# Shifting the weight tiles of a layer's first half by 384 bytes in SBUF

## The chip, the cores and the metric

The kernel runs on one NeuronCore of a Trainium2 chip. The metric is the device time of one execution in microseconds (us); three executions before the change took 1393.44 to 1394.48 us, with a median of 1394.12 us.

## What is computed

One layer of a trunk, `x + W_out [ya, yb, yc]`, with 256 tokens and 4096 channels in float32. The three branches read the same normalised input through one combined input projection, and a final RMSNorm follows.

```python
h = _rmsnorm(x, norm_g[l])
proj = h @ w_in[l]                       # 256 x 4096 by 4096 x 11008
a_val, a_glu, a_gate, b_u, b_v, b_gate, c_in, c_gate = jnp.split(proj, SPLITS, axis=-1)
ya = _conformer_conv_branch(...) * jax.nn.silu(a_gate)   # 31 taps, LayerNorm, 1536 x 1536
yb = _gmlp_chunk_branch(...) * jax.nn.silu(b_gate)       # position mixing per head
yc = _pool_branch(...) * jax.nn.silu(c_gate)             # trailing means, 320 x 320 per group
y = jnp.concatenate([ya, yb, yc], axis=-1) @ w_out[l]    # 256 x 4096 by 4096 x 4096
x = x + y
return _rmsnorm(x, final_g)
```

## The kernel before

Each operand of a large product is split into two parts, `hi` (rounded to the type that TensorE multiplies, `F32R`) and `lo` (the rest), and a product is the sum of three matmuls, `act_hi x w_hi`, `act_hi x w_lo` and `act_lo x w_hi`. In `rows_product` these are lines 338, 339 and 340. The activations are the stationary operand: tiles `act` of 2048 bytes in each partition, in which hi and lo of the two halves of the tokens lie 512 bytes apart. The weights are the moving operand, 512 columns at a time in most places.

`stream` (called from `project_rows`) reads weights in blocks of 1 MB into `w_raw` tiles on the SP queue (L205), and `split` makes of every 1024 columns the `w_hi` part (ScalarE, L218) and the `w_lo` part (VectorE, L219). `feed` keeps two split pairs ahead of the pair that TensorE multiplies; one pair serves twelve matmuls of 512 columns. Beside each split, `run_beside` records some of the elementwise work of the branches (convolution L525, gates, norms), so the order on each engine is fixed when the program is built.

The program has two halves, by where the weights lie in SBUF:

- **First half**: `first_group`, the other column groups of the input projection, the C branch's small products (`use_c`, 320 columns wide) and the A branch's pointwise projection. Its weight tiles come from the pool `wpool` at the right end of SBUF: four `w_raw` of 8192 bytes, three `w_hi` and three `w_lo` of 4096 bytes. The branch tiles `h_a` and `a_gate` lie in the pool `gate`, to the left of it.
- **Second half**: `first_columns` (the first 512 columns of the output projection, by the same `stream` and the same lines 338 to 340, into the same PSUM pool `ps_acc`), then three times `paired_columns` (products L875 to L877 into the banks `q`), then the last 512 columns (`use_last`, again L338 to L340, in the order 512, 256, 256 columns at first). Its weight tiles come from the pool `wpool2` on the left, right behind the activations, with three `w_raw` and five `w_hi` and `w_lo` each.

The activations lie in the same 32 places in both halves. Byte addresses in a partition, as the built program has them:

| tiles | address | modulo 512 | modulo 2048 |
|---|---|---|---|
| `act` (32 tiles, step 2048; four parts of 512 bytes each) | 19552 to 83040 | 96 | 1120 |
| `w_hi`, `w_lo` of the first half, before | 204768 to 225248, step 4096 | 480 | 2016 |
| `w_hi`, `w_lo` of the first half, after | 204384 to 224864, step 4096 | 96 | 1632 |
| `w_hi`, `w_lo` of the second half, before and after | 109664 to 146528, step 4096 | 96 | 1120 |
| `w_raw` of the first half, before and after | 172000 to 196576; 171616 to 196192 | 480; 96 | 2016; 1632 |
| `h_a`, `a_gate`, before and after | 158272; 157888 | 64; 192 | 576; 192 |

So a weight part of the first half lies 384 bytes past a multiple of 512 from every activation part before the change; one of the second half lies at a multiple of 512 from them, and since the four parts of an `act` tile are 512 bytes apart, all four distances modulo 2048 (0, 512, 1024, 1536) occur there.

Of the 512-column products, the first half holds 1416 at each of the lines 338, 339 and 340 (4248 matmuls); 64 at each of these lines belong to `first_columns` and 32 to the last columns. The matmuls of 256 columns are 64 at each line in the first half (the last chunk of `b_v`) and 64 in the last columns.

Of the kernel before, what the change touches and what calls it, by code (L numbers as in the profile page):

```python
# [22 lines left out]
F32 = mybir.dt.float32  # L23
# [5 lines left out]
P = 128  # L29
# [65 lines left out]
def trunk(ctx: ExitStack, tc: tile.TileContext, x, xt, params, w1, wv, w2, w_pw, w_c, w_o, wst, bbias, blg, blb, fg, out):  # L95
# [3 lines left out]
    acts = ctx.enter_context(tc.tile_pool(name="acts", bufs=1))  # L99

    front_ctx, ps_ctx = ExitStack(), ExitStack()
    weights = {"pool": front_ctx.enter_context(tc.tile_pool(name="wpool", bufs=1, side="right")), "raw": 4, "parts": 3}
    gate = front_ctx.enter_context(tc.tile_pool(name="gate", bufs=1, side="right"))
    ps_acc = ps_ctx.enter_context(tc.tile_pool(name="ps_acc", bufs=6, space=PSUM))
# [1023 lines left out]
```

## Time and profile before

| what | value |
|---|---|
| median of three executions | 1394.12 us |
| the profiled execution | 1392.27 us, span 1390.5 us |
| TensorE busy | 99% of the span, 6224 records |
| VectorE busy | 75% |
| ScalarE busy | 49% |
| granted TensorE clock | 1.00 of full speed, 0.88 in the last of 40 slices |
| moved by DMA | 281 MB, 202 GB/s in the mean |

PE is TensorE, PEld its loads of the stationary operand, DVE VectorE, ACT ScalarE, POOL GpSimd, SP the queue that issues most DMAs. L339 is line 339 of the kernel. The matmuls are pipelined: the duration of a record is longer than the step from one start to the next, and steps are what the time is made of.

### The profile page before, as it was taken

How to read it: one execution, taken by the hardware profiler on the slowest of the kernel's cores; microseconds unless marked ns; L12 is line 12 of the kernel's file. 1: busy time of each engine (PE TensorE's matmuls, PEld its weight loads, DVE VectorE, ACT ScalarE, POOL GpSimd, SP SyncE). 2: the span in 40 equal slices, each digit the busy share in tenths (PEclk: the TensorE clock that was granted, in tenths of full speed). 3: DMA queues.
4: the chain of work that ended last, by engine and by line, in shares of the span. 5: the costliest groups of instructions: out<-in, count | busy, mean ns of one | idle time of the engine just before them, and what ended most of it. 6: DMA issues, size and time to landing. Idle time of an engine off the chain costs nothing.

```text
span 1390.5 us, 16340 instructions
## 1 busy us (share of the span) xinstructions
PE 1378.2 (99%) x6224; PEld 1133.2 (81%) x6224; DVE 1036.0 (75%) x1468; ACT 675.7 (49%) x806; POOL 5.7 (0%) x52
## 2 busy tenths in 40 slices
PE   9999999999999999999999999999999999999996
PEld 7888888888888888888888888888888888888886
DVE  7458888888888888776445844456668999999974
ACT  7653444434445434554344334445554565655651
POOL 0000000000000000000000000000000000000000
PEclk9999999999999999999999999999999999999998
DMA  9965555555556555555555555554656666666663
GB/s 341 335 255 186 195 182 182 185 185 199 187 195 195 190 198 183 182 182 185 176 183 182 184 190 197 187 181 135 225 212 219 232 214 218 215 212 210 225 224 121
DMA packets 56591, 281.01 MB, mean 202 GB/s; under 512 B 8640, under 2 KB 12096, under 8 KB 31168
## 3 DMA queue, kind: packets, MB, share of 16 engines
q1 hardware_dynamic: 56368, 279.95, 57.5%
q8 instruction: 48, 0.79, 0.2%
q14 instruction: 31, 0.25, 0.0%
q10 hardware_dynamic: 144, 0.02, 0.0%
HBM read 275.75 MB, written 4.19 MB: 201 GB/s over the span
## 4 chain that ended last, share of the span: by engine, by line
PE 99%; DVE 1%; ACT 0%; issue 0%; POOL 0%; ACTq 0%; POOLq 0%
PE ps_acc L338 25%; PE ps_acc L339 25%; PE ps_acc L340 25%; PE q L875 6%; PE q L876 6%; PE q L877 6%; PE q L339 1%; PE q L338 1%; PE q L340 1%; PE ps_aux L315 1%; PE ps_aux L391 0%; PE ps_aux L613 0%; PE ps_aux L276 0%; DVE xn L999 0%; ACT ps_acc L841 0%; DVE w_lo L219 0%
## 5 line engine op out<-in xcount | busy, mean ns | idle before, releaser
L219 DVE TENSOR_TENSOR w_lo<-w_raw,w_hi 128x1024 fp32r<-128x1024 f32 (+1 forms) x495 | 589.0, 1195 | 307.5 <-ACT w_hi L218 305.9
L218 ACT CAST w_hi<-w_raw 128x1024 fp32r<-128x1024 f32 (+1 forms) x495 | 505.0, 1027 | 581.9 <-PE ps_acc L340 506.5
L338 PE MATMUL ps_acc<-w_hi,act 128*128 128x512 f32 (+2 forms) x1568 | 611.9, 391 | 0.0
L339 PE MATMUL ps_acc<-w_lo,act 128*128 128x512 f32 (+2 forms) x1568 | 610.6, 389 | 0.0
L340 PE MATMUL ps_acc<-w_hi,act 128*128 128x512 f32 (+2 forms) x1568 | 610.4, 389 | 0.0
L339 PEld LDWEIGHTS ps_acc<-w_lo,act 128*128 128x128 f32 x1568 | 295.7, 189 | 64.5 <-DVE w_lo L219 0.8
L340 PEld LDWEIGHTS ps_acc<-w_hi,act 128*128 128x128 f32 x1568 | 295.6, 189 | 64.4
L338 PEld LDWEIGHTS ps_acc<-w_hi,act 128*128 128x128 f32 x1568 | 295.6, 189 | 64.2 <-ACT act L295 0.4
L525 DVE SCALAR_TENSOR_TENSOR c_a<-h_a,par,c_a 128x256 f32<-128x256 f32 x360 | 153.5, 477 | 0.0
L875 PE MATMUL q<-w_hi,act 128*128 128x512 f32 x264 | 102.9, 390 | 0.7 <-ACT ps_acc L841 0.7
L876 PE MATMUL q<-w_lo,act 128*128 128x512 f32 x264 | 102.8, 389 | 0.0
L877 PE MATMUL q<-w_hi,act 128*128 128x512 f32 x264 | 102.8, 389 | 0.0
L218 ACT CAST w_hi<-w_sums 128x1024 fp32r<-128x1024 f32 x48 | 50.6, 1054 | 56.3 <-DVE w_sums L950 28.5
L219 DVE TENSOR_TENSOR w_lo<-w_sums,w_hi 128x1024 fp32r<-128x1024 f32 x48 | 58.1, 1220 | 2.6 <-ACT w_hi L218 1.7
L875 PEld LDWEIGHTS q<-w_hi,act 128*128 128x128 f32 x264 | 49.6, 188 | 11.5 <-ACT ps_acc L841 1.2
L877 PEld LDWEIGHTS q<-w_hi,act 128*128 128x128 f32 x264 | 49.6, 188 | 10.3
L876 PEld LDWEIGHTS q<-w_lo,act 128*128 128x128 f32 x264 | 49.6, 188 | 10.2
L877 PE MATMUL q<-w_hi,combo 128*128 128x512 f32 x96 | 37.4, 389 | 0.0
L876 PE MATMUL q<-w_lo,combo 128*128 128x512 f32 x96 | 37.4, 389 | 0.0
L875 PE MATMUL q<-w_hi,combo 128*128 128x512 f32 x96 | 37.0, 389 | 0.0
L339 PE MATMUL q<-w_lo,act 128*128 128x256 f32 (+1 forms) x96 | 30.7, 320 | 0.0
L338 PE MATMUL q<-w_hi,act 128*128 128x256 f32 (+1 forms) x96 | 30.7, 319 | 0.0
(147 smaller groups left out, 614.8 us busy)
## 6 DMA issues: line engine op xcount, KB each, us to landing
w_raw<-in_w_dram SPq DMA_DIRECT2D x149, 1024.0 KB, 4.8
w_raw<-in_w_o_dram SPq DMA_DIRECT2D x96, 512.0 KB, 4.8
w_raw<-in_wv_dram SPq DMA_DIRECT2D x20, 1024.0 KB, 4.8
w_raw<-in_w_o_dram SPq DMA_DIRECT2D x16, 1024.0 KB, 5.1
w_raw<-in_w_pw_dram SPq DMA_DIRECT2D x9, 1024.0 KB, 4.8
x_rows<-in_x_dram SPq DMA_DIRECT2D x4, 1024.0 KB, 6.7
xn<-in_x_dram SPq DMA_DIRECT2D x8, 512.0 KB, 8.1
out_dram<-xn SPq DMA_DIRECT2D x6, 512.0 KB, 3.3
```

The costliest lines, as they stand in the source:

```text
L218: nc.scalar.copy(out=hi[:, w], in_=raw[:, w])
L219: nc.vector.tensor_tensor(out=lo[:, w], in0=raw[:, w], in1=f32(hi[:, w]), op=ALU.subtract)
L315: nc.tensor.transpose(ps[:, c * P : (c + 1) * P], rows[:, c, m * P : (m + 1) * P], ident)
L338: nc.tensor.matmul(ps[:, :w], lhsT=act[:, c, 0], rhs=hi, start=f, stop=False)
L339: nc.tensor.matmul(ps[:, :w], lhsT=act[:, c, 0], rhs=lo, start=False, stop=False)
L340: nc.tensor.matmul(ps[:, :w], lhsT=act[:, c, 1], rhs=hi, start=False, stop=l)
L525: nc.vector.scalar_tensor_tensor(out=c_a[:, m], in0=src, scalar=w, in1=c_a[:, m], op0=ALU.mult, op1=ALU.add)
L875: nc.tensor.matmul(ps, lhsT=ahi, rhs=hi, start=f, stop=False)
L876: nc.tensor.matmul(ps, lhsT=ahi, rhs=lo, start=False, stop=False)
L877: nc.tensor.matmul(ps, lhsT=alo, rhs=hi, start=False, stop=l)
```

## The change

One tile of 96 float32 (384 bytes in each partition) is taken at the right end of SBUF before the weight pool. Nothing reads or writes it.

```diff
     front_ctx, ps_ctx = ExitStack(), ExitStack()
+    ctx.enter_context(tc.tile_pool(name="edge", bufs=1, side="right")).tile([P, 96], F32, name="edge")
     weights = {"pool": front_ctx.enter_context(tc.tile_pool(name="wpool", bufs=1, side="right")), "raw": 4, "parts": 3}
     gate = front_ctx.enter_context(tc.tile_pool(name="gate", bufs=1, side="right"))
```

What stands at the right end, `wpool` and `gate`, moves down by 384 bytes; nothing else moves. The two built programs have the same 10083 instructions in the same order with the same waits; the addresses alone differ.

## Rows read from the trace of the kernel before

**Rows 1.** The page: engines' busy time, and the chain that ended last by engine.
```profile
PE 1378.2 (99%) x6224; PEld 1133.2 (81%) x6224; DVE 1036.0 (75%) x1468; ACT 675.7 (49%) x806; POOL 5.7 (0%) x52
...
PE 99%; DVE 1%; ACT 0%; issue 0%; POOL 0%; ACTq 0%; POOLq 0%
```

**Rows 2.** Stretches: us, busy time and records of each engine, clock, DMA share, GB/s.
```profile
core 0: us, PE busy (x) PEld busy (x) DVE busy (x) ACT busy (x) POOL busy (x), PEclk, DMA share, GB/s
105.00:345.00 240.00, 240.00 (x1043) 194.94 (x1042) 198.98 (x322) 100.30 (x104) 0.00 (x0) 1.00 0.53 186
800.00:940.00 140.00, 140.00 (x604) 113.61 (x603) 67.67 (x62) 58.35 (x61) 0.00 (x0) 1.00 0.53 188
1050.00:1088.00 38.00, 38.00 (x169) 31.51 (x168) 32.28 (x65) 17.95 (x21) 0.00 (x0) 1.00 0.81 279
1110.00:1250.00 140.00, 140.00 (x619) 116.00 (x618) 135.41 (x150) 83.40 (x93) 0.00 (x0) 1.00 0.63 214
```

**Rows 3.** Line 339 from 800 to 940 us: ns min/median/max.
```profile
L339 PE MATMUL ps_acc<-w_lo,act x202: 390/393/405, 799.7 to 939.9; 128*128 128x512 f32 x101
```

**Rows 4.** Line 339 from 1050 to 1088 us, in `first_columns`: ns min/median/max.
```profile
L339 PE MATMUL ps_acc<-w_lo,act x57: 388/389/390, 1049.7 to 1087.8; 128*128 128x512 f32 x57
```

**Rows 5.** Groups of TensorE, whole span, shapes apart: xcount | busy us, mean ns.
```profile
L338 PE MATMUL ps_acc<-w_hi,act 128*128 128x512 f32 x1480 | 586.0, 397 | 0.0
...
L338 PE MATMUL q<-w_hi,act 128*128 128x256 f32 x64 | 18.1, 282 | 0.0
L338 PE MATMUL ps_acc<-w_hi,act 128*128 128x256 f32 x64 | 18.0, 282 | 0.0
...
L391 PE MATMUL ps_aux<-ident,hv 128*128 128x128 f32 x44 | 5.8, 272 | 0.0
L613 PE MATMUL ps_aux<-v,ws_sb 128*128 128x256 f32 x20 | 5.7, 389 | 0.0
...
L315 PE MATMUL ps_aux<-ident,a_gate 128*128 128x128 f32 x24 | 4.6, 274 | 0.0
L315 PE MATMUL ps_aux<-ident,c_gate 128*128 128x128 f32 x20 | 4.1, 278 | 0.0
L315 PE MATMUL ps_aux<-ident,u_b 128*128 128x128 f32 x20 | 3.0, 272 | 0.0
```

**Rows 6.** Timeline of TensorE behind a stall in `paired_columns`: start us, us, instruction.
```profile
1091.20 0.51 PE L875 MATMUL q<-w_hi,act 128*128 128x512 f32 x1 [0.74 <-ACT ps_acc L841]
1091.55 0.40 PE L876 MATMUL q<-w_lo,act 128*128 128x512 f32 x1
...
1094.33 0.39 PE L876 MATMUL q<-w_lo,act 128*128 128x512 f32 x1
...
1095.91 0.39 PE L877 MATMUL q<-w_hi,act 128*128 128x512 f32 x1
```

**Rows 7.** Groups of TensorE from 1340 to 1362 us, shapes apart.
```profile
L338 PE MATMUL q<-w_hi,act 128*128 128x512 f32 x16 | 6.3, 396 | 0.0
```

**Rows 8.** Timeline of TensorE in the first half, from 826 us.
```profile
826.00 0.40 PE L338 MATMUL ps_acc<-w_hi,act 128*128 128x512 f32 x1
826.24 0.41 PE L339 MATMUL ps_acc<-w_lo,act 128*128 128x512 f32 x1
826.48 0.40 PE L340 MATMUL ps_acc<-w_hi,act 128*128 128x512 f32 x1
```

**Rows 9.** Waits in the first 45 us: us in total, times, longest.
```profile
ACT w_hi L218 <- DMA w_raw<-in_w_dram: 6.4, 6, 2.0
ACT w_hi L218 <- PE ps_acc L340: 4.0, 3, 1.8
```

**Rows 10.** Waits from 105 to 1044 us.
```profile
ACT w_hi L218 <- PE ps_acc L340: 463.1, 280, 4.5
DVE w_lo L219 <- ACT w_hi L218: 248.3, 241, 2.4
...
PEld ps_acc L339 <- DVE w_lo L219: 0.3, 1, 0.3
```

**Rows 11.** Groups of VectorE from 105 to 345 us: xcount | busy us, mean ns | idle before.
```profile
L219 DVE TENSOR_TENSOR w_lo<-w_raw,w_hi 128x1024 fp32r<-128x1024 f32 x86 | 105.3, 1225 | 40.4 <-ACT w_hi L218 40.1
```

**Rows 12.** Line 525, the convolution, all of it: ns min/median/max.
```profile
L525 DVE SCALAR_TENSOR_TENSOR c_a<-h_a,par,c_a x360: 413/478/483, 102.2 to 545.7; 128x256 f32<-128x256 f32 x180
```

## The prediction

> **What bounds the kernel now.** First the page: TensorE is busy 99% of the span and 99% of the chain that ended last, while VectorE and ScalarE have 25% and 51% of the span free [rows 1]. So time can only go if TensorE gets more matmuls into a microsecond. Next, who waits for whom: from 105 to 1044 us ScalarE's split waits 280 times, 463.1 us, for TensorE to release a `w_hi` part, VectorE waits behind ScalarE, and the one wait of TensorE for a split in that list is 0.3 us [rows 10]. The helpers follow TensorE, not the other way round. Last, whether TensorE keeps one pace everywhere. It does not. A record counts in a stretch when any part of it lies there, so n records cover the stretch plus about one record's 0.39 us. From 800 to 940 us, in the first half, 140.39 us / 604 = 232.4 ns from one 512-column matmul to the next; from 1110 to 1250 us, in the second half, 140.39 / 619 = 226.8 ns; the granted clock is 1.00, the level of 2.4 GHz, in both [rows 2]. Records say the same: line 339 has 390 to 405 ns (median 393) in the one, and 388 to 390 in `first_columns` from 1050 to 1088 us [rows 3, 4].
>
> **Whose doing is the 5.6 ns?** `first_columns` runs the same lines on the same shape, from activation tiles in the same places, into the same PSUM pool. What differs is where the weight tiles lie (384 against 0 bytes past a multiple of 512 from the activations), how many there are, and what runs beside. The last can be judged: the slow stretch is the quiet one (VectorE 67.67 of 140 us, DMA share 0.53), the fast ones are the busy ones (VectorE 135.41 of 140 us; DMA share 0.81 in `first_columns`) [rows 2]. In the first half the pace does not follow the load either: with VectorE busy 198.98 of 240 us there are 1043 records in 240.39 us, 230.5 ns each with a few short transposes among them [rows 2]. More pairs in store cannot speed up a TensorE that waits for none. The address remains.
>
> **The change part by part.** It adds no instruction and takes none; every address of `wpool` and `gate` falls by 384 bytes, and the weights then lie at 96 modulo 512, as the activations do and as the second half's weights do.
>
> - *Matmuls of 512 columns in the first half.* 1480 records of line 338 [rows 5], less the 64 of `first_columns`, are 1416, at three lines 4248 matmuls. At 232.4 - 226.8 = 5.6 ns each that is 23.8 us. Bounds: nothing (the address has no part in it), and 6 ns (the difference of the usual 395 and 389 ns of a record), 25.5 us. I take 5.6, because the second half holds all four distances modulo 2048 that the change makes, and its records spread over no more than 388 to 390 ns [rows 4].
> - *Matmuls of 256 columns.* 282 ns in the first half (distance 384) and 282 ns in the last columns (distance 0) [rows 5]: nothing to gain on 192 of them. The 72 of 320 columns I leave at nothing too; 5.6 ns on each would be 0.4 us.
> - *Finding the fast pace again.* After a stall the second half does not run at 226.8 ns at once. From 1091.55 to 1094.33 us twelve steps took 2.78 us, 232 ns each; from 1094.33 to 1095.91 seven took 226 ns each [rows 6]. And where six matmuls of 512 columns alternate with twelve of 256, line 338 stays at 396 ns though the distance is 0 [rows 7]. So each interruption should cost up to 14 matmuls x 5 ns = 0.07 us of the gain. The first half has some 53: 44 transposes of L391 in fours, 64 of L315 in pairs, 10 matmuls of L613 (two records each) [rows 5], that is 11 + 32 + 10. Bounds 0 and 3.7 us; I take the middle, 1.8 us, since a pair of transposes disturbs less than a stall of 0.74 us.
> - *What must keep up.* From 105 to 345 us VectorE is the nearest: 198.98 of 240 us, 83% [rows 2]; with TensorE 2.4% faster 85%. Its splits sit idle 40.1 us there behind ScalarE [rows 11], which is cover enough. The next late thing is the one 0.3 us wait for `w_lo` [rows 10]; I add 0.2 us. In the first 45 us ScalarE waits 6.4 us for weights from DMA and 4.0 us for TensorE [rows 9]: about the first 12 us belong to the transfers and keep their length, worth some 50 matmuls x 5.6 ns = 0.3 us less gain. Cover gone in the whole of this start (the first group of 192 matmuls) would take 1.1 us.
> - *VectorE and ScalarE at the new addresses.* `h_a` moves against `c_a`. The taps already read it at 31 starts four bytes apart, and 360 instructions stay within 413 to 483 ns [rows 12], so nothing. `w_raw`, `w_hi` and `w_lo` move together.
>
> Sum: 23.8 - 1.8 - 0.2 - 0.3 = 21.5 us. The profiled execution has 1392.27 us, so 1370.8 us for such a one; the median before is 1.85 us above it, and from 1394.12 us I forecast **1372.6 us**.
>
> **The rivals.**
>
> *No change, 1394 us (chance 0.07).* The two halves differ in more than addresses: five against three parts in store, and `w_raw` on the other side of SBUF. If one of these sets the pace, the first half stays at 232.4 ns. For it: the 396 ns of [rows 7] show that distance 0 alone does not make the fast pace. Against it: TensorE waits for no part [rows 10], and those slow matmuls stand between others of 256 columns, which the first half has only in one chunk. The Trainium skill takes this rival's side: its page "SBUF — State Buffer" (section "Who interferes with whom") gives TensorE two independent read ports, one for the moving operand and one for weight loads, and says that it never waits on anyone; by that, the place of the weights is free and the time stays at 1394 us. The rows at two paces speak against that rule so far, but none varies the address alone.
>
> *A part of the gain, 1380 to 1388 us (chance 0.06).* The first half might fall out of the fast pace more often than the interruptions count, or the distance modulo 2048 of each part and its neighbour might matter. At a third to half of the 23.8 us the time is about 1382 to 1386 us. Against it: the flat 388 to 390 ns [rows 4].
>
> *Slower, 1426 us (chance 0.04).* In the first half steps of 0.24 us stand between steps of 0.23 [rows 8]. If the new place held every matmul at the long step instead of the short one, each would pay 0.24 - 0.2324 = 7.6 ns, and 4248 of them 32 us: 1394 + 32 = 1426 us. It decides as soon as the mean step of the first half is over 232.4 ns. For it: a step that depends on the meeting of two reads can lock on either side. Against it: the second half at the same distances locks on the short one.
>
> **How the numbers follow.** The forecast has 0.83. Faster by over 0.2% (2.8 us, what a measurement of this kernel can tell from no change): 0.83 and the partial gain's 0.06, 0.89. Within 0.2%: 0.07. Slower: 0.04. The range's low end is the 6 ns bound with nothing lost, 1394.1 - 25.5 = 1368.6, taken down to 1368 for the spread of the runs; the high end takes both losses at their worst (23.8 - 3.7 - 0.2 - 1.1 - 0.4 leaves 18.4 us, 1375.7) and reaches into the partial gain, 1380.
>
> **What would show it.** Right: from 800 to 940 us about 618 records instead of 604, line 339 at 388 to 390 ns there, the start of `first_columns` about 21 us earlier, the second half unchanged in length, no new wait of TensorE. Wrong: 604 records there again (the first rival), or a flat pace with waits of PEld for `w_lo` in the stretches where VectorE is busiest. If the pace is flat but the total gain is under 18 us, the term on interruptions was too small.

## The result, and the profile after

The changed kernel takes 1370.05 us (median of four executions, 1369.99 to 1371.58) against 1394.26 us before (four, 1393.44 to 1394.48): a ratio of 0.983, with a 95% interval of 0.9813 to 0.9847, some 24 us less. The forecast was 1372.6 us in a range of 1368 to 1380 us. The profiled executions are 1371.58 us (span 1369.9 us) and 1392.27 us, 20.7 us apart; of the changed kernel's four executions the profiled one was the longest.

The stretches of the changed kernel's trace, with the columns of [rows 2]; the last two lie 24 us earlier than their counterparts there, since the second half now begins 20.7 us earlier. Four short transposes are among the 172 records of the third.

```profile
core 0: us, PE busy (x) PEld busy (x) DVE busy (x) ACT busy (x) POOL busy (x), PEclk, DMA share, GB/s
105.00:345.00 240.00, 240.00 (x1069) 198.90 (x1068) 201.82 (x329) 102.79 (x106) 0.00 (x0) 1.00 0.54 190
800.00:940.00 140.00, 140.00 (x620) 115.95 (x619) 73.56 (x76) 64.87 (x76) 0.00 (x0) 1.00 0.55 192
1026.00:1064.00 38.00, 38.00 (x172) 31.42 (x171) 31.52 (x64) 18.48 (x22) 0.00 (x0) 1.00 0.77 252
1086.00:1226.00 140.00, 140.00 (x620) 115.91 (x619) 135.65 (x147) 85.23 (x96) 0.00 (x0) 1.00 0.63 212
```

From 800 to 940 us TensorE now has 620 records instead of 604, the same as from 1086 to 1226 us in the second half: 140.39 us / 620 = 226.4 ns against 232.4 before. The granted clock is 1.00 in all four, as it was. The product with the lo part, line 340 now, has the records of the second half in the first, 389 to 390 ns where [rows 3] had 390 to 405:

```profile
L340 PE MATMUL ps_acc<-w_lo,act x207: 389/389/390, 799.8 to 939.9; 128*128 128x512 f32 x104
```

The starts of the matmuls in the two traces show where the time went. `first_columns` began at 1044.52 us and now begins at 1023.86 us; from there to the last matmul it is 335.19 and 335.15 us. All of the gain lies in the first half. The first 51 us give none of it in these two executions: the 192nd matmul of 512 columns started at 51.27 us before and at 51.43 us now. The usual steps are shorter there too (what those under 300 ns have over 226.67 ns falls from 1.3 to 0.15 us in sum), but the steps of 300 ns and more, in which TensorE waits, grow from 3.1 to 5.1 us. ScalarE's first split of weights starts at 6.54 us now and at 5.99 us before, behind a wait for the transfer. In the traces of four other kernels below whose first half is fast (activations moved, parts alone, second half slow, 256 bytes) the 192nd starts between 50.28 and 51.68 us, so one execution does not tell what the start gains.

One wait has grown. The list of waits of the changed kernel from 395 to 430 us:

```profile
DVE v L607 <- DMA gb<-in_blb_dram: 3.3, 2, 2.6
DVE v L605 <- DMA gb<-in_blg_dram: 2.0, 2, 1.8
...
PEld ps_acc L340 <- DVE w_lo L220: 1.6, 1, 1.6
PE ps_acc L340 <- DVE w_lo L220: 1.1, 1, 1.1
```

VectorE waits here for the gains and offsets of `norm_v`, and a split is queued behind. In [rows 10] the same wait is 0.3 us. From start to start this step of TensorE took 0.33 us before and takes 1.54 us here, 1.2 us more. Only a part of that comes from TensorE's arriving earlier: in the traces of the same four kernels the step takes 0.41 to 0.70 us, and the longest wait for `in_blg_dram` is 1.8 us here and was 1.1 us before.

### The profile page after: what moved, and what is told of

It is laid out like the page before. It is cut to its first block, busy times and chain, and to the rows that moved or that the text cites. A ratio compares the mean times of both kernels' runs of the same rounds, so it can differ in the third digit from the quotient of the medians.

```text
span 1369.9 us, 16340 instructions
## 1 busy us (share of the span) xinstructions
PE 1355.4 (99%) x6224; PEld 1129.4 (82%) x6224; DVE 1033.1 (75%) x1468; ACT 676.9 (49%) x806; POOL 5.7 (0%) x52
## 4 chain that ended last, share of the span: by engine, by line
PE 96%; DMA 2%; DVE 1%; ACT 0%; issue 0%; SPq 0%; ACTq 0%; DVEq 0%
PE ps_acc L340 25%; PE ps_acc L341 25%; PE ps_acc L339 25%; PE q L876 6%; PE q L878 6%; PE q L877 6%; PE q L339 1%; PE q L340 1%; PE q L341 1%; DMA w_raw<-in_w_dram 1%; DMA gb<-in_blb_dram 1%; DVE w_lo L220 1%; PE ps_aux L316 1%; PE ps_aux L392 0%; PE ps_aux L614 0%; ACT w_hi L219 0%
## 5 line engine op out<-in xcount | busy, mean ns | idle before, releaser
L340 PE MATMUL ps_acc<-w_lo,act 128*128 128x512 f32 (+2 forms) x1568 | 602.7, 384 | 1.8 <-DVE w_lo L220 1.8
L339 PE MATMUL ps_acc<-w_hi,act 128*128 128x512 f32 (+2 forms) x1568 | 603.9, 386 | 0.3 <-ACT act L296 0.3
L341 PE MATMUL ps_acc<-w_hi,act 128*128 128x512 f32 (+2 forms) x1568 | 602.7, 384 | 0.0
```

What stands on the lines that cost most here:

```text
L339: nc.tensor.matmul(ps[:, :w], lhsT=act[:, c, 0], rhs=hi, start=f, stop=False)
L340: nc.tensor.matmul(ps[:, :w], lhsT=act[:, c, 0], rhs=lo, start=False, stop=False)
L341: nc.tensor.matmul(ps[:, :w], lhsT=act[:, c, 1], rhs=hi, start=False, stop=l)
```

## Experiments: what has to lie where

Each experiment has 4 to 10 executions beside 13 to 24 of the kernel before on the same chip (the last experiment has one of each). Of most, one row is shown: the stretch from 800 to 940 us, in the first half, where the column groups run on without an interruption. The theory to begin with was the prediction's: the distance between the moving weights and the stationary activations, modulo 512 bytes, sets the pace.

**The activations moved instead of the weights.**

```diff
+    ctx.enter_context(tc.tile_pool(name="edge", bufs=1)).tile([P, 96], F32, name="edge")
     acts = ctx.enter_context(tc.tile_pool(name="acts", bufs=1))
```

> The 384 bytes are put ahead of the activations on the left instead, and the weights of the first half stay at 480 modulo 512; the activations come to 480 too, so the distance is 0 at another absolute place. Theory (the distance between moving and stationary rows modulo 512 sets the pace): as the changed kernel, 1370 us, with 619 to 620 records from 800 to 940 us. Rival (the weights' own address counts, 480 is slow and 96 is fast): the first half stays at 604 records and the second half, whose weights come to 480 as well, turns slow: 1394 us plus 1368 matmuls x 5.6 ns = 1402 us.

1370.82 us, ratio 0.9837 (0.9822 to 0.9851).

```profile
800.00:940.00 140.00, 140.00 (x619) 115.95 (x618) 74.37 (x76) 64.28 (x77) 0.00 (x0) 1.00 0.54 191
```

With both at 480 modulo 512 it is as fast as with both at 96, and the second half, where both are at 480 now too, keeps 619 records from 1086 to 1226 us. Between these two places the weights' own address does not count; the distance does.

**The split parts alone, and the raw tiles alone.** `w_hi` and `w_lo` get a pool of their own at the right end, and gaps ahead of it and behind it move the one or the other.

```diff
+    ctx.enter_context(tc.tile_pool(name="edge", bufs=1, side="right")).tile([P, 96], F32, name="edge")
+    split_pool = front_ctx.enter_context(tc.tile_pool(name="wparts", bufs=1, side="right"))
+    front_ctx.enter_context(tc.tile_pool(name="gap", bufs=1, side="right")).tile([P, 32], F32, name="gap")
```

(The other kernel has no `edge`, and 96 in place of 32.)

> Only w_hi and w_lo move by 384 bytes; a further gap of 128 bytes keeps w_raw, h_a and a_gate at their old places modulo 512. Theory: 1370 us, 620 records from 800 to 940 us. Rival (where w_raw and the branch tiles lie is what counted, through ScalarE, VectorE or the DMAs): 1394 us, 604 records.

1369.81 us, ratio 0.983 (0.9816 to 0.9845):

```profile
800.00:940.00 140.00, 140.00 (x619) 115.97 (x618) 74.48 (x76) 64.13 (x76) 0.00 (x0) 1.00 0.54 191
```

> The opposite: w_raw, h_a and a_gate move by 384 bytes, w_hi and w_lo stay 384 bytes past a multiple of 512 from the activations. Theory: 1394 us, 604 records from 800 to 940 us. Rival (the raw tiles' place counts): 1370 us, 620 records.

1393.56 us, ratio 0.9999 (0.999 to 1.0008):

```profile
800.00:940.00 140.00, 140.00 (x604) 113.52 (x603) 67.94 (x62) 57.92 (x60) 0.00 (x0) 1.00 0.52 188
```

The whole gain follows `w_hi` and `w_lo`. What ScalarE and VectorE read and where the DMAs write the raw weights, and the branch tiles `h_a` and `a_gate`, have no part in it.

**The second half made slow.**

```diff
+    back(name="shift").tile([P, 96], F32, name="shift")
     weights.update(pool=back(name="wpool2"), raw=3, parts=HELD)
```

> The changed kernel with 384 bytes put ahead of the second half's weight pool, so that there too the weights lie 384 bytes past a multiple of 512 from the activations; the sums of activations (combo) move along and stay at a multiple of 512 from the weights. Theory: the products with act, 1080 of 1368 matmuls of 512 columns, go to 232.4 ns, those with combo stay at 226.8: 1370 + 1080 x 5.6 ns = 1376 us; line 340 in first_columns at 393 ns, line 877 with act at about 393 and with combo at 389. Rival (the number of parts and the side set the pace of the second half): 1370 us and 389 ns everywhere.

(The `edge` tile of the changed kernel is in this one as well.)

1377.12 us, ratio 0.9891 (0.9874 to 0.9907), 7.1 us over the changed kernel. The stretch from 1086 to 1226 us, in `paired_columns`, where the changed kernel has 620 records, and TensorE's groups in it (xcount | busy us, mean ns):

```profile
1086.00:1226.00 140.00, 140.00 (x605) 113.63 (x605) 132.75 (x144) 84.23 (x94) 0.00 (x0) 1.00 0.59 203
```

```profile
L878 PE MATMUL q<-w_lo,act 128*128 128x512 f32 x142 | 56.1, 395 | 0.0
...
L879 PE MATMUL q<-w_hi,combo 128*128 128x512 f32 x60 | 23.6, 394 | 0.0
L878 PE MATMUL q<-w_lo,combo 128*128 128x512 f32 x60 | 23.4, 390 | 0.0
L877 PE MATMUL q<-w_hi,combo 128*128 128x512 f32 x59 | 23.0, 393 | 0.0
```

The same code that ran at 389 ns everywhere is slow once its weights lie 384 bytes off, so neither five parts in store nor the left side made it fast. One line of the expectation was wrong: the products with `combo`, whose distance stays 0, did not keep 389 ns but have 390 to 394. They stand in runs of twelve between slow products. By the starts in the trace the first step of such a run takes 235 ns in the mean and the ninth to eleventh 227 to 228 ns: the pace takes some matmuls to come back.

**Only `w_lo` off.** (`w_lo` has its own pool at the right end, 96 float32 between it and the rest.)

> In the first half w_hi lies at a multiple of 512 from the activations, w_lo 384 bytes past one (w_raw moves with w_hi). Theory A (each matmul pays for its own distance): line 340 keeps 232.4 ns and the other two run at 226.8, so 1370 + 1416 x 5.6 ns = 1378 us, 614 records from 800 to 940 us. Theory B (the pace is a state that a sequence falls into, which every third matmul breaks): nearly all of the loss, 1386 to 1394 us, 604 to 609 records.

1391.28 us, ratio 0.9982 (0.9973 to 0.9991):

```profile
800.00:940.00 140.00, 140.00 (x607) 113.80 (x606) 68.47 (x63) 58.34 (x63) 0.00 (x0) 1.00 0.54 190
```

607 records, 231.3 ns: theory B. Two of three products at distance 0 gain little when the third is off: 2.5 of some 24 us. By the starts from 800 to 940 us, the mean step behind the three products is 230.9 ns (`act_hi x w_hi`), 229.6 (`act_hi x w_lo`, the one that lies off) and 232.9 (`act_lo x w_hi`). A matmul does not pay for its own distance; the sequence has a pace.

## Experiments: which distances

**256, 128 and 64 bytes.** Only the size of the tile differs from the changed kernel: 32, 64 and 80 float32 instead of 96.

> A tile of 128 bytes instead of 384: the weights of the first half lie 256 bytes past a multiple of 512 from the activations. Runs so far allow two periods, since 384 is slow and all multiples of 512 are fast: 512 and 256 bytes. Theory (512): slow, 1388 to 1400 us, 598 to 607 records from 800 to 940 us. Rival (256 is enough): 1370 us, 620 records.

1369.74 us, ratio 0.9825 (0.9808 to 0.9841):

```profile
800.00:940.00 140.00, 140.00 (x620) 115.91 (x619) 74.29 (x78) 64.93 (x78) 0.00 (x0) 1.00 0.54 189
```

This fells the theory's period: a distance of 256 is as good as one of 512, so the change did not need "a multiple of 512".

> A tile of 256 bytes: distance 128. Theory (two reads that step along in lockstep meet in the same places unless they lie a multiple of 512 apart): slow as the kernel before, 1394 us, about 604 records from 800 to 940 us, if the loss does not depend on how far apart the places are; a rival in which nearness counts would put 128 between 0 and 256, some 1378 to 1388 us and 608 to 615 records.

1393.42 us, ratio 0.9998 (0.9989 to 1.0007):

```profile
800.00:940.00 140.00, 140.00 (x602) 112.63 (x601) 67.41 (x61) 57.90 (x60) 0.00 (x0) 1.00 0.53 188
```

> A tile of 320 bytes: distance 64. Theory (nearness does not count): 1394 us, 604 records from 800 to 940 us. Rival (nearness counts): nearer to the changed kernel than at distance 128, 1372 to 1380 us, 614 to 619 records.

1377.61 us, ratio 0.988 (0.9865 to 0.9895):

```profile
800.00:940.00 140.00, 140.00 (x614) 114.86 (x613) 72.06 (x71) 62.11 (x71) 0.00 (x0) 1.00 0.55 194
```

128 is slow and 64 lies between, which looked as if nearness to a multiple of 256 counted. Three more distances were to test that.

**32, 96 and 192 bytes** (88, 72 and 48 float32).

> Distance 32 (a tile of 352 bytes). Theory now (period 256, and the loss grows with the distance to the nearest multiple of 256: 0 at 0 and 256, 2.2 ns at 64, about 6 ns at 128 and 384): about 1 ns per matmul, 1371 to 1375 us, 616 to 619 records from 800 to 940 us. Rival (steps: nothing up to some distance, then all): 1370 us and 620 records, or 1377 us and 614.

1396.01 us, ratio 1.0018 (1.0009 to 1.0027):

```profile
800.00:940.00 140.00, 140.00 (x601) 112.46 (x601) 67.41 (x61) 57.96 (x60) 0.00 (x0) 1.00 0.54 188
```

> Distance 96 (a tile of 288 bytes). Theory: between 64 and 128, about 4 ns per matmul, 1382 to 1389 us, 607 to 611 records from 800 to 940 us. Rival (steps): 1377 us and 614 records, or 1393 us and 602 to 604.

1396.73 us, ratio 1.0024 (1.0014 to 1.0034):

```profile
800.00:940.00 140.00, 140.00 (x601) 112.62 (x601) 67.06 (x59) 57.81 (x60) 0.00 (x0) 1.00 0.54 188
```

> Distance 192 (a tile of 192 bytes), which is 64 before a multiple of 256. Theory (the same to either side): as distance 64, 1377.6 us, 614 records from 800 to 940 us. Rival (which of the two reads lies ahead counts): not as 64 but near the slow ones, 1388 to 1394 us, 602 to 607 records, or near 1370 us.

1396.44 us, ratio 1.0023 (1.0013 to 1.0033):

```profile
800.00:940.00 140.00, 140.00 (x602) 112.80 (x601) 67.40 (x60) 57.88 (x61) 0.00 (x0) 1.00 0.53 188
```

Nearness falls at once, and at 32 neither the theory nor its rival came true: 32 bytes away from the best place is slower than the kernel before. By the starts from 800 to 940 us the mean step is 233.3 ns at 32, 96 and 192 bytes, against 232.4 before. 64 is an exception, not a point on a slope, and 192 is not its mirror image.

**All in one kernel.** Each column group of the first half puts its parts at another place in larger tiles.

```diff
+            weights["pool"].tile([P, SUB + room], F32R, tag=t, name=f"w_{t}_{d}b" if room else f"w_{t}", bufs=weights["parts"])[:, at : at + SUB]
```

> One kernel with many distances: the weight tiles of the first half get 512 bytes more each, and every column group puts its parts at another place in them, so that its matmuls (192 of 512 columns for most) run at one distance; tiles are named after it (w_lo_32b). Distances 0 (first group), 16, 32, 48, 64, 80, 96, 112, 8, 128, 144, 160, 176, 192, 208, 224, 240, 256, 320, 4, 272, and 504 and 0 in the pointwise projection. Theory 1 (period 256; only multiples of 256 are fast, 64 past one is a case between): records of line 340's kind (the lo product) 389 ns at 0 and 256, 391 to 392 at 64 and 320, 393 to 396 at all others, also at 4, 8 and 16. Theory 2 (two reads within 16 bytes of each other share what they wait for): 4, 8, 16, 240 and 504 are fast as well. Theory 3 (64 is special and 256 too, period 512): 320 at 394 to 396. The time is the sum over the groups: some 18 of 22 full groups slow, 1388 to 1394 us by theory 1, some 4 to 6 us less by theory 2.

1389.89 us, beside 1394.77 us, one execution of each. The lo product's records by the tile's name, which carries the distance (duration ns min/median/max, first and last start; each row is one group of 64):

```profile
L346 PE MATMUL ps_acc<-w_lo_4b,act x64: 390/399/403, 885.8 to 930.6; 128*128 128x512 f32 x64
...
L346 PE MATMUL ps_acc<-w_lo_80b,act x64: 392/392/392, 230.3 to 274.0; 128*128 128x512 f32 x64
...
L346 PE MATMUL ps_acc<-w_lo_128b,act x64: 392/395/398, 432.8 to 476.9; 128*128 128x512 f32 x64
L346 PE MATMUL ps_acc<-w_lo_144b,act x64: 394/394/397, 477.6 to 521.7; 128*128 128x512 f32 x64
...
L346 PE MATMUL ps_acc<-w_lo_256b,act x64: 389/389/398, 798.3 to 841.1; 128*128 128x512 f32 x64
...
L346 PE MATMUL ps_acc<-w_lo_320b,act x64: 388/388/397, 841.8 to 885.1; 128*128 128x512 f32 x64
```

The last of 64 starts is 189 steps behind the first. At 256 bytes that is 42.8 us / 189 = 226.5 ns; at 320, 43.3 / 189 = 229.1; at 128 and 144, 44.1 / 189 = 233.3; at 4 bytes, the slowest, 44.8 / 189 = 237.0. From the starts in the trace, with steps of 300 ns and more and the four steps behind a transpose left out, the means are:

| distance in bytes | ns from matmul to matmul |
|---|---|
| 0, 256 | 227.1, 226.8 |
| 64, 320 | 228.9, 229.0 |
| 208 | 230.0 |
| 80, 112, 16, 272 | 231.1, 231.1, 231.6, 231.7 |
| 504, 176, 240 | 232.2, 232.6, 233.0 |
| 8, 32, 48, 96, 128, 144, 192, 224 | 233.3 to 233.4 |
| 160, 4 | 234.2, 237.2 |

Theory 1 holds in its main part: 0 and 256 are the fast ones, 320 repeats 64, and 4, 8, 16 and 504 are slow, which ends theory 2; 320 ends theory 3. It had the records of one line wrong: at 64 and 320 the lo product has 388 ns, and the other two products carry the loss. And "all others slow" was too coarse, with 208, 80, 112, 16 and 272 in between. The total alone would not have told theory 1 from theory 2, whose ranges overlap at 1389.89 us; the rows by distance do. Most distances stand here on one group in one execution; 32, 64, 96 and 192 have the same step in kernels of their own.

## Why the prediction was right

- **TensorE's pace sets the time, and the address sets its pace: right.** Moving the parts alone gives the whole gain, moving the rest alone gives none. The rival of no change stood on what else differs between the halves; the second half made slow ends it. Of the partial gain nothing came: from 800 to 940 us every step has 225 to 228 ns.
- **The rule of the Trainium skill on the ports.** The Trainium skill's page "SBUF — State Buffer" (section "Who interferes with whom") has TensorE's moving operand and its weight loads on independent ports and TensorE waiting on no one. Taken to mean that the place of its operands is free, it would have given 1394 us. Here it did not hold: the parts' place alone is worth 24 us. Whether a read waits at all, and which of the two, no run shows.
- **The main term, 4248 x 5.6 ns = 23.8 us: right.** Against a step of 226.67 ns the first half's steps of 512 columns (those under 300 ns, some 4210) were 24.5 us too long in the trace before and are 1.0 us too long in the trace after. That is 23.5 us.
- **Finding the pace again, 1.8 us: too large.** That last 1.0 us is all that losing the pace costs in the first half, the start's share of 0.15 us included. The pace is lost behind a stall as the prediction says: behind the step of 1.54 us at 420 us sixteen steps of 231.3 ns follow in the mean. But behind the transposes at 98.7 us only two steps (232 and 231 ns) are long. The fourteen matmuls behind the stall in [rows 6] were no measure of a pair of transposes.
- **256 columns: nothing to gain, right.** The 64 records of the first product have 283 ns now, 282 before [rows 5]. Their steps, by the starts in the first half, went from 118.7 to 120.0 ns, so 192 of them lost about 0.25 us.
- **The start and the waits, 0.5 us: too small for the profiled execution.** The first 51 us gained nothing (the bound of 1.1 us) and the wait behind `gb` grew by 1.2 us, of which the prediction had 0.2. The other three executions of the changed kernel are 1.5 us shorter than the profiled one, and in four other fast kernels that wait is much shorter, so about that much changes from run to run.
- **The sum: near, in part by luck.** The faster steps gave 23.5 us where 23.8 - 1.8 = 22.0 us were forecast, and start, wait and 256 columns took some 2.7 us where 0.5 were forecast. The two errors offset each other in the profiled executions: 20.7 us, forecast 21.5. Between the medians of four the gain is 24.2 us. Beside the larger samples of the kernel before (medians of 1393.67 and 1393.78 us), the three fast kernels with the second half as it was (activations moved, parts alone, 256 bytes) gain 22.9 to 24.0 us, so some 23.5 us, 2 us more than the forecast.
- **VectorE keeps up: right.** From 105 to 345 us it is busy 201.82 us, 84%, where 85% was forecast.
- **The rival on the slower side** does not happen at this distance, and no run comes near its 1426 us. Slower places exist, though: at 32, 96 and 192 bytes the mean step is 233.3 ns, 0.9 ns over the kernel before where the rival had 7.6, and the time is 1396 to 1397 us. The kernel before was not at the worst place.
- **The period in the argument was wrong, without harm.** The prediction named 512 because the second half showed four multiples of 512; 256 is enough.

## What to carry to other kernels

Where TensorE is the bound and waits for nothing, compare its pace between stretches that run the same shape: a difference of some percent that follows no engine's load is worth a look at where the operands lie. For 512 columns of 4 bytes with a weight load before each matmul, a multiple of 256 bytes between the moving and the stationary operand was the best of the places tried, and every product of the sequence had to lie so: with one of three 384 bytes off, nine tenths of the gain were gone. A tile of padding is a free edit, but one that moves well-placed operands apart costs about as much per matmul as the right one gains, so scan the places rather than reason about nearness.

## What the runs showed of the hardware

The means are not spread evenly. 226.67, 228.89, 231.11 and 233.33 ns are a base and one, two and three thirds of 6.67 ns more, and the kernel before, at 232.4, lies 6/7 of it above the base. 6.67 ns are 16 cycles at 2.4 GHz, the level that the granted clock of 1.00 means. In steady stretches the single steps repeat in a short pattern. At 64 bytes it is 226, 229, 232: the starts below, which the view rounds to 10 ns, are 826.211, 826.437, 826.666 and 826.898 us in the trace.

```profile
826.21 0.39 PE L339 MATMUL ps_acc<-w_hi,act 128*128 128x512 f32 x1
826.44 0.39 PE L340 MATMUL ps_acc<-w_lo,act 128*128 128x512 f32 x1
826.67 0.39 PE L341 MATMUL ps_acc<-w_hi,act 128*128 128x512 f32 x1
826.90 0.39 PE L339 MATMUL ps_acc<-w_hi,act 128*128 128x512 f32 x1
```

At one distance there can be more than one pattern: at 128 bytes the mean step is 232.4 ns from 100 to 340 us and 233.3 from 800 to 940 us of one execution, and at 240 bytes in the kernel with many distances the second to twelfth steps take 226 to 228 ns until four transposes come between, and the steps behind those 233.3 in the mean. So the distance seems to decide which patterns can hold, and what went before decides which one does; that is an inference from these means, not a thing that a run took apart.

The weight loads are nearly as long at every pace: from 800 to 940 us 115.95 us / 619 = 187.3 ns in the changed kernel, 113.61 / 603 = 188.4 before [rows 2] and 112.46 / 601 = 187.1 ns at 32 bytes. What grows, by the starts and ends in the trace from 800 to 940 us, is the gap between the end of a load and the start of the next matmul: 34 to 37 ns in the changed kernel, 40 to 45 at 32 bytes. That does not tell which read is held up.

For 256 columns the order is another: the lo product's records in the first half have 279 ns at distance 32, 280 at 64 and 283 at 0 and 256, and the steps are 116.7, 117.8 and 120.0 ns. What is best for one width is not best for all.

Open: whether the address of a matmul's own stationary operand counts or that of the next load, since nearly every step here has the same distance to both; and why 64 and 208 are better than their neighbours.
